# Hand-set waits and fixed buffers in place of a scheduler's pools, in a store-heavy batched product kernel

## Chip, cores, metric

The kernel runs on one core of one Trainium2 chip. The metric is the device time of one execution in microseconds (us), as the median of several. The engines are called TensorE (PE), VectorE (DVE), ScalarE (ACT), GpSimd (POOL) and SyncE (SP). SyncE only issues transfers. SBUF is the on-chip memory that transfers read and write, PSUM the memory that TensorE writes its products to.

## The reference

```python
def reference(x, y):            # both (8, 12, 512, 64), float32
    return np.einsum('bhtc,bhsc->bhts', x, y).astype(np.float32)   # (8, 12, 512, 512)
```

Two inputs of 12.6 MB each become 100.7 MB of output. Nothing can be stored in less than 125.83 MB of traffic in all.

## The kernel before

The inputs come in 12 loads of 2 MB (x and y of six groups of 16 heads), are cast to bf16 and rearranged by ScalarE, VectorE and GpSimd, and are transposed on VectorE. Then come 48 results of 2 MB each. A result is two groups of four products into one of two PSUM halves, two copies (evictions) by ScalarE into a slot in SBUF, and one store by SyncE. Five slots serve the loads and the stores in turn. A scheduler's pools hand out the buffers, and the scheduler sets the waits; the order is the program's. Cut to what matters:

```python
    slots = ctx.enter_context(tc.tile_pool(name="slots", bufs=SLOTS))   # SLOTS = 5
    tpool = ctx.enter_context(tc.tile_pool(name="tpool", bufs=2))
    pmpool = ctx.enter_context(tc.tile_pool(name="pmpsum", bufs=2, space=bass.MemoryType.PSUM))
    # ...
    def result(o, otf):                                   # otf: a slot
        i, h = divmod(o, V)
        xT, yT = made[i]
        ot = otf.rearrange("p (r s) -> p r s", s=S)
        for k in range(0, K, 4):
            pm = pmpool.tile([P, 4, S], fp32)
            for j in range(4):
                nc.tensor.matmul(pm[:, j, :], xT[:, k + j, h, :], yT[:, h * S:(h + 1) * S], start=True, stop=True)
            copy(nc.scalar, ot[:, k:k + 4, :], pm)
        nc.sync.dma_start(ov[i, h], otf)
    # ...
    with tc.manual_schedule():
        for g in range(SLOTS):
            load(g)
        for half, engine, part in ((0, nc.vector, 256), (1, nc.gpsimd, 128)):
            for k in range(0, K * E * D, part):
                engine.memset(zeroed[half][:, k:k + part], 0.0)
        # ... the front: 12 loads converted, results 0 to 3 among them
        for o in range(V, V * NH):                        # results 4 to 47
            result(o, slot())
            if o % V == V - 1:
                prepare(o // V + 2)                       # next transposes and rearrangements
```

## Time and profile before

| before | value |
|---|---|
| time, median of the 3 first runs | 301.13 us (301.11 to 301.54) |
| span of the profiled run | 299.4 us |
| TensorE / VectorE / ScalarE / GpSimd busy | 46 / 52 / 71 / 19 % |
| DMA engines busy by the kernel's queue | 98.8 % |
| read / written | 25.17 / 100.66 MB |

The table is read from the bottom: the busy share of every compute engine is far from 100, that of the DMA engines is not. The prediction shows the lines behind it. Here are only two more of the page before, of its third part (queue and kind: packets, MB, share of the 16 engines' span). They are the engines' own instructions, which are fetched by DMA too:

```profile
q8 instruction: 3, 0.05, 0.1%
q14 instruction: 3, 0.02, 0.0%
```

### The profile page before, as it was taken

The numbers are of one execution on the slowest core, as the hardware profiler recorded it, in microseconds if no ns is written. First come the engines' busy times: TensorE is split into PE (matmuls) and PEld (weight loads), VectorE is DVE, ScalarE is ACT, GpSimd is POOL, SyncE is SP. The second block draws the span as 40 slices with busy tenths as digits, with TensorE's granted clock in tenths as the row PEclk, the third lists the DMA queues.
The fourth block names the chain that finished last, engine by engine and source line by source line (L and its number), as shares of the span: only waits on it lengthen the run. The fifth ranks groups of instructions, "written<-read, shape, count | busy, mean of one in ns | idle before, by whom it ended". The sixth has DMA issues, their size and how long they took to land.

```text
span 299.4 us, 1218 instructions
## 1 busy us (share of the span) xinstructions
PE 136.7 (46%) x377; PEld 45.3 (15%) x384; DVE 154.5 (52%) x80; ACT 211.8 (71%) x109; POOL 56.6 (19%) x38
## 2 busy tenths in 40 slices
PE   0000130555665555746666466657465756465000
PEld 0000010111222221212112122212121212121000
DVE  2259996999749592916719359086192520000000
ACT  1756576999999978686867777777777686868100
POOL 3399989991000000000000000000000000000000
PEclk9999999978799997595677776677787577676555
DMA  7999999999999999999999999999999999999995
GB/s 282 431 433 429 429 427 431 429 425 436 431 427 433 431 425 430 440 424 427 440 425 427 442 422 429 437 425 431 427 431 429 425 429 425 429 422 427 429 431 219
DMA packets 8646, 125.91 MB, mean 421 GB/s; under 512 B 960, under 2 KB 960, under 8 KB 960
## 3 DMA queue, kind: packets, MB, share of 16 engines
q1 hardware_dynamic: 8640, 125.83, 98.8%
q8 instruction: 3, 0.05, 0.1%
q14 instruction: 3, 0.02, 0.0%
HBM read 25.17 MB, written 100.66 MB: 420 GB/s over the span
## 4 chain that ended last, share of the span: by engine, by line
DMA 55%; ACT 21%; DVE 7%; issue 5%; PE 2%; ACTq 1%; SPq 0%
DMA out_dram<-slot 48%; ACT slot L66 20%; DMA slot<-in_y_dram 7%; DVE yb L68 6%; PE pm L133 2%; DVE xT L115 1%; ACT yb L66 1%; ACTq L201 1%; DVE yT L120 1%; SPq L75 0%; ACTq L66 0%; ACT xk L83 0%
## 5 line engine op out<-in xcount | busy, mean ns | idle before, releaser
L66 ACT ACTIVATE slot<-pm 128x2048 f32<-128x2048 f32 x96 | 174.2, 1887 | 44.0 <-DMA out_dram<-slot 42.3
L133 PE MATMUL pm<-yT,xT 128*128 128x512 bf16 x377 | 136.7, 504 | 137.9 <-ACT slot L66 100.8
L115 DVE STREAM_TRANSPOSE xT<-xb 128x2048 uint32<-128x2048 uint32 x12 | 46.7, 3894 | 68.4 <-PE pm L133 68.3
L133 PEld LDWEIGHTS <-xT 128*128 128x128 bf16 x384 | 45.3, 118 | 228.5 <-issue 177.8
L68 DVE COPY xb<-xk 32x2048 bf16<-32x2048 bf16 x36 | 46.9, 1303 | 0.5
L68 DVE CAST yb<-slot 64x2048 bf16<-64x2048 f32 x12 | 38.5, 3204 | 16.8 <-DMA slot<-in_y_dram 16.6
L68 POOL COPY xb<-xk 32x2048 bf16<-32x2048 bf16 x12 | 37.3, 3107 | 9.6 <-ACT xk L83 8.9
L83 ACT ACTIVATE xk<-slot 128x4096 bf16<-128x4096 f32 x6 | 21.7, 3617 | 16.1 <-DMA slot<-in_x_dram 16.1
L120 DVE STREAM_TRANSPOSE yT<-yb 128x1024 uint32<-128x1024 uint32 x12 | 23.1, 1927 | 0.0
L66 ACT ACTIVATE yb<-slot 64x2048 bf16<-64x2048 f32 x6 | 14.8, 2462 | 5.1 <-DMA slot<-in_y_dram 5.1
L68 POOL CAST yb<-slot 64x2048 bf16<-64x2048 f32 x6 | 16.8, 2808 | 1.5 <-DMA slot<-in_y_dram 1.4
L152 DVE MEMSET xb<- 128x256 uint32 x8 | 2.2, 272 | 0.9 <-PEq L190 0.9
L152 POOL MEMSET xb<- 128x128 uint32 x16 | 2.3, 210 | 0.3 <-POOLq L190 0.3
L83 ACT ACT_TABLE_LOAD x1 | 1.3, 1283 | 0.7 <-PEq L190 0.7
L190 POOL MEMSET const-float32-0.0<- 128x1 f32 x1 | 0.1, 98 | 0.2 <-issue 0.2
L190 POOL MEMSET const-float32-1.0<- 128x1 f32 x1 | 0.1, 98 | 0.0
L190 POOL MEMSET const-bfloat16-1.0<- 128x1 bf16 x1 | 0.1, 98 | 0.0
L190 POOL MEMSET const-uint8-127<- 128x1 uint8 x1 | 0.1, 98 | 0.0
## 6 DMA issues: line engine op xcount, KB each, us to landing
out_dram<-slot SPq DMA_DIRECT2D x48, 2048.0 KB, 20.6
slot<-in_x_dram SPq DMA_DIRECT2D x6, 2048.0 KB, 16.4
slot<-in_y_dram SPq DMA_DIRECT2D x6, 2048.0 KB, 20.8
```

The lines of the kernel that those rows point to most:

```text
L66: nc.scalar.activation(dst, src, COPY)
L68: engine.tensor_copy(dst, src)
L83: nc.scalar.activation(xk.rearrange("p r c -> p (r c)"), src, COPY)
L115: nc.vector.transpose(xT.rearrange("p (k r e) -> p k e r", k=K, e=E), xb.rearrange("p (k e c) -> p k e c", k=K, e=E),)
L120: nc.vector.transpose(yT.rearrange("p (r j) -> p j r", r=D), yb.rearrange("p (j c) -> p j c", c=D))
L133: nc.tensor.matmul(pm[:, j, :], xT[:, k + j, h, :], yT[:, h * S:(h + 1) * S], start=True, stop=True)
L152: engine.memset(zeroed[half][:, k:k + part], 0.0)
L190: nc = _bacc.Bacc("TRN2", target_bir_lowering=False, num_devices=1)
L201: with _tile.TileContext(nc) as tc:
```

## The change

The intent is to wait for less. Each instruction says what it reads and writes; a small bookkeeping finds the points it depends on, drops those that its engine already knows to be past (also by way of another engine's knowledge), and sets the remaining waits by hand. The buffers are fixed and numbered. Each slot has its own DMA count. The two zeroings become one instruction each, results 43 and 47 are copied by VectorE, and everything stands in one section which the scheduler treats as a unit. All stores remain with SyncE. The core of the diff:

```diff
-    slots = ctx.enter_context(tc.tile_pool(name="slots", bufs=SLOTS))
-    pmpool = ctx.enter_context(tc.tile_pool(name="pmpsum", bufs=2, space=bass.MemoryType.PSUM))
+    slots = [sb.tile([P, K * S], fp32, name=f"slot{i}") for i in range(SLOTS)]
+    pms = [ps.tile([P, 4, S], fp32, name=f"pm{i}") for i in range(2)]
     # ... the same for all other buffers
+    def need(name, points):
+        best = {}
+        for p, v in points:
+            if known[name].get(p, 0) < v:
+                best[p] = max(best.get(p, 0), v)
+        for p, v in list(best.items()):
+            if any(snaps[q, w].get(p, 0) >= v for q, w in best.items() if q != p):
+                del best[p]
+        for p, v in best.items():
+            engines[name].wait_ge(sems[p], v)
+            known[name][p] = v
+            for q, w in snaps[p, v].items():
+                known[name][q] = max(known[name].get(q, 0), w)
     # ...
     def slot():
-        return slots.tile([P, K * S], fp32, name="slot")
+        made_slots.append(len(made_slots) % SLOTS)
+        return made_slots[-1]
     # ...
-            copy(nc.scalar, ot[:, k:k + 4, :], pm)
-        nc.sync.dma_start(ov[i, h], otf)
+            copy("dve" if o in late else "act", ot[:, k:k + 4, :], pms[pm], [("pm", pm)], [("slot", s, pm)])
+        store(o, s)                       # late = results 43 and 47
     # ...
-    with tc.manual_schedule():
+    with tc.tile_critical():
     # ...
+        for i, name in enumerate(("dve", "pool", "dve", "pe", "act")):
+            need(name, [(f"dma{i}", ticks[f"dma{i}"])])
```

## The prediction

> **What bounds the kernel now.** I began with the page's totals and its slices in time, because they say at once whether any engine can be the bound over the whole span. The slices' last two rows, and the DMA queue's row:
>
> ```profile
> DMA  7999999999999999999999999999999999999995
> GB/s 282 431 433 429 429 427 431 429 425 436 431 427 433 431 425 430 440 424 427 440 425 427 442 422 429 437 425 431 427 431 429 425 429 425 429 422 427 429 431 219
> ...
> q1 hardware_dynamic: 8640, 125.83, 98.8%
> ```
>
> The DMA engines are 90% busy or more in 38 of 40 slices; the first and the last slice alone are lower. No compute engine comes near: ScalarE, the busiest, has 211.8 us of 299.4 (71%). The one queue moves 125.83 MB. At the 430 GB/s of the long middle stretch (second listing, line 110 to 270) that is 125.83 / 0.430 = 292.6 us. So 292.6 of 299.4 us is bytes over a fixed rate, and 6.8 us is all that any change which keeps the bytes can touch.
>
> Where these 6.8 us lie I read from busy time by stretch, at the two ends (columns: stretch, its length, PE, PE load, VectorE, ScalarE, GpSimd busy with counts, granted clock, DMA share, GB/s):
>
> ```profile
> 0.00:1.00 1.00, 0.00 (x0) 0.00 (x0) 0.14 (x1) 0.27 (x1) 0.47 (x6) 1.00 0.00 0
> 1.00:2.00 1.00, 0.00 (x0) 0.00 (x0) 0.99 (x5) 1.00 (x1) 1.00 (x9) 1.00 0.95 180
> ...
> 50.00:70.00 20.00, 10.44 (x24) 3.24 (x24) 17.13 (x7) 19.68 (x11) 17.49 (x6) 0.83 1.01 428
> 70.00:90.00 20.00, 11.73 (x39) 4.18 (x40) 14.25 (x7) 19.77 (x12) 0.00 (x0) 0.91 1.00 429
> ...
> 110.00:270.00 160.00, 96.72 (x257) 31.45 (x260) 71.97 (x40) 118.45 (x66) 0.00 (x0) 0.71 1.01 430
> ...
> 290.00:295.00 5.00, 0.00 (x0) 0.00 (x0) 0.00 (x0) 0.00 (x0) 0.00 (x0) 0.50 0.99 419
> 295.00:298.00 3.00, 0.00 (x0) 0.00 (x0) 0.00 (x0) 0.00 (x0) 0.00 (x0) 0.50 0.26 109
> 298.00:299.40 1.40, 0.00 (x0) 0.00 (x0) 0.00 (x0) 0.00 (x0) 0.00 (x0) 0.50 0.00 0
> ```
>
> The start loses about 2.6 us: no byte in the first microsecond, then a ramp. The end loses about 3.8 us: from 295 to 298 only a quarter of the DMA engines still work, and from 298.3 the closing barrier runs. I also followed the landings of the last store over its 16 DMA engines as the trace records them: first at 295.82, last at 298.31 us. One engine lags by 2.5 us, and the kernel ends 1.08 us after it.
>
> Next the waits of the issuing queue, to see which waits the change could take away:
>
> ```profile
> SPq L137 <- ACT slot L66: 204.4, 48, 10.8
> SPq L75 <- DVE yb L68: 26.6, 3, 11.1
> SPq L201 <- DMA out_dram<-slot: 20.0, 1, 20.0
> ```
>
> SyncE waits 204.4 us for evictions, which looks like a bound and is not one. A store is issued while its predecessors are still in the DMA rings, and lands a median 20.6 us after issue, although 2 MB take only 2.097 / 0.430 = 4.88 us of the engines. So about four transfers are queued ahead of each store. The evictions wait for landings in turn:
>
> ```profile
> ACT slot L66 <- DMA out_dram<-slot: 42.3, 34, 1.7
> ```
>
> ScalarE is thus paced by the stores and not the stores by ScalarE. In the chain that ended last, stores carry 48% and evictions 20%: both halves of the ring of five slots, whose period in the second half is 20.8 us of landing plus 3.7 us of eviction, 24.5 us for five stores of 4.9 us each.
>
> **What the Trainium skill says.** "DMA: Bandwidth & Descriptors", section Specifications, gives a fabric ceiling of 435 GB/s for the 16 engines together. The trace agrees: 430 GB/s in the middle, 99% of it, for loads (4 to 50 us: 431) and stores alike. The same page, section Issuing engines are not separate DMA queues, says that transfers from all engines run on the same 16 DMA engines. So even the stores' place of issue would be no lever; here it stays SyncE anyway. "Runtime: NRT & Kernel Launch", section Instruction fetch mechanics, says that sequencers fetch instructions by DMA in 16 KiB blocks. The trace shows three packets of 16 KiB on one instruction queue, at 100, 174 and 253 us, and three of 8 KiB on another, smaller than the page's block. The packet at 100 us took 0.96 us, and the spread of landings went from 0.65 to 1.86 us there: these fetches make the lag at the end. For the late VectorE copies, "Perfetto Trace Analysis", section Optimizing Scalar/DVE Operations, gives some 125 ns of access overhead on PSUM for VectorE. No VectorE copy from PSUM is in this trace.
>
> **The change part by part.**
>
> 1. Waits by hand. In the built programs SyncE's instructions that only wait fall from 63 to 8, since each store after the third waited for an older transfer's count as well as for ScalarE. Such an instruction takes 17 ns by its record. Fifty-five of them are below 55 x 0.06 = 3.3 us of dispatch even at the 61 ns spacing the trace shows for back-to-back ones, and all lie inside the 204 us that SyncE idles. The older counts had been reached long before. ScalarE's go from 55 to 50, TensorE's rise from 3 to 13, VectorE's stay 17. On the path: 0.
>
> 2. Fixed buffers. Five slots, two products' halves in PSUM, two sets of transposed inputs, five or six kept ones: the same numbers in the same rotation, and the instruction order on all engines is the same but for the two points below. On the path: 0.
>
> 3. Zeroing in one instruction instead of 8 and 16. It ends by 3.1 us before; the first load lands at 8.3 us. On the path: 0.
>
> 4. The evictions of results 43 and 47 go to VectorE. VectorE's memset of 256 four-byte columns takes 272 ns in the trace; eight times that is 2.2 us, and with the page's overhead I estimate 2.3 us each against ScalarE's 1.88, so a store is issued about 0.8 us later. Ahead of it lie four transfers, 19.5 us. On the path: 0.
>
> 5. Entry to and exit from the hand-synchronized section. SyncE signals and branches once more before the first load: two sequencer instructions and a semaphore hop. The same kind of steps are about 60 ns apart in the trace, and SyncE needed 85 ns from barrier to first load; so +0.15 us, wholly on the path, as every byte moves with it. At the end five SyncE waits at 61 ns (0.31 us) go away. In their place come ScalarE's branch and drain, one hop, then two waits, a no-op and a branch on SyncE: six or seven steps, 0.4 us. So +0.1 us.
>
> 6. Instruction fetches. TensorE's listed instructions fall from 776 to 405, because a weight load is no longer a separate entry. I expect the machine program to have both as before, hence the same three 16 KiB fetches. SyncE's fall from 129 to 79, so one 8 KiB fetch may vanish or move: 8 KiB take 0.31 us of one engine, if it is the lagging one. -0.1 us on average.
>
> Sum: +0.15 + 0.1 - 0.1 = +0.15 us, so 301.13 + 0.15, rounded to 301.3 us.
>
> **The rivals.**
>
> First rival: the queue runs dry in the front. Between 54 and 90 us evictions and input conversions share ScalarE, which is busy 19.7 of 20 us in both stretches above. I took each store's issue against the first landing of its predecessor: at 68.0 us the cover is 3.5 us, at 78.0 us only 3.1 us, less the 1.0 us that lies between issue and first packet at the start. So 2 us of slack are left, where the steady state has 17. If a hand-set wait on GpSimd or VectorE delays the front by 3 us, the time rises by 1 us; a delay of 8 us, which would cost 2%, has no source in the diff. For it: GpSimd now waits for itself before each step. Against: ScalarE's order and durations there are unchanged, and the transposes on VectorE wait for TensorE or for casts there and not for GpSimd. It would make 302 to 303.
>
> Second rival: TensorE becomes the bound, if the weight loads can no longer run beside the products. 8 loads x 118 ns = 0.94 us per store, on top of 8 x 0.504 = 4.0 us at the average clock: 4.97 us against 4.88. That would add up to 0.1 us x 40 stores = 4 us in the worst case, but four queued transfers absorb it until late. Against it: ScalarE's wait for TensorE is 1.6 us in total now. It would make at most 303.
>
> Third rival: the waits removed were worth something, as the intent of the change suggests. Then the DMA engines would have to show gaps in the middle; they show 1.00 to 1.01 of share. Only the 6.8 us at the ends remain, and nothing in the diff shortens the ramp; an end with less lag could give 0.5 to 1 us. It would make 300.2.
>
> **Range and chances.** The three runs before lie within 0.43 us. With the lag at the end (up to 1 us either way) and the front rival upward, 300.4 to 302.3 should hold it 8 times in 10. Faster by over 2% means under 295.1, 5.9 of the 6.8 us that are not bytes: 1%. Slower by over 2% means over 307.2: 2%. Within 2%: 97%.
>
> **What would show it.** DMA share of 0.99 or more in all stretches from 4 to 290 us, and 430 GB/s; SyncE's wait for evictions again some 200 us although its wait instructions are gone; the first load issued at about 0.9 instead of 0.74 us; about 1.2 instead of 1.08 us from the last landing to the end; four VectorE copies of some 2.3 us near the end with nothing waiting for them. It is wrong if the DMA row shows a hole between 55 and 95 us (first rival), if ScalarE's wait for TensorE grows to tens of microseconds (second), or if the middle stretch moves more than 431 GB/s (then the rate, and not the waiting, had changed).

## The result, and the profile after

The changed kernel takes 300.99 us (median of 4 runs, 300.72 to 301.31); the kernel before, in the same rounds, 301.12 us (4 runs, 300.98 to 301.54). The ratio is 0.9994, 95% interval 0.9976 to 1.0011: the same. (A ratio here is the mean time of one kernel's fast runs over the mean of the other's of the same rounds, so not quite the ratio of the medians quoted.)

The slices' last two rows and the queues, from the page after:

```profile
DMA  7999999999999999999999999999999999999995
GB/s 270 430 430 438 425 425 427 434 427 430 427 438 427 430 432 432 429 427 432 434 427 435 430 430 430 430 430 427 434 430 423 430 434 419 432 423 425 430 434 248
...
q1 hardware_dynamic: 8640, 125.83, 98.9%
q8 instruction: 3, 0.05, 0.1%
q14 instruction: 2, 0.02, 0.0%
```

The row of the DMA engines is digit for digit that of before. One 8 KiB packet of instructions is gone from the second instruction queue. Busy time by stretch after, with the columns of the prediction's listing:

```profile
50.00:70.00 20.00, 9.99 (x24) 2.49 (x24) 17.28 (x7) 19.71 (x10) 18.10 (x6) 0.59 1.00 427
70.00:90.00 20.00, 11.69 (x41) 3.43 (x40) 13.97 (x7) 19.74 (x12) 0.00 (x0) 0.89 1.01 432
...
110.00:270.00 160.00, 98.69 (x260) 25.18 (x260) 76.88 (x42) 114.78 (x64) 0.00 (x0) 0.70 1.01 430
...
295.00:298.00 3.00, 0.00 (x0) 0.00 (x0) 0.00 (x0) 0.00 (x0) 0.00 (x0) 0.50 0.28 120
298.00:299.00 1.00, 0.00 (x0) 0.00 (x0) 0.00 (x0) 0.00 (x0) 0.00 (x0) 0.50 0.00 0
```

The middle stretch moves 430 GB/s again, and the front stretches have no hole. The waits of SyncE after (waited for: us in total, times, longest):

```profile
SPq L211 <- ACT slot L112: 189.4, 46, 6.6
...
SPq L211 <- DVE slot L114: 10.7, 2, 5.5
```

Together 200.1 us for 48 stores, against 204.4: SyncE has 55 fewer wait instructions and waits as long as before, since what it waits for comes no sooner. ScalarE still waits 45.2 us for stores to land (before 42.3).

What moved lies at the ends. First the issue of the first load, in the timeline of before and then of after (start, duration, engine, line, operation):

```profile
0.74 0.39 SPq L75 DMA_DIRECT2D slot<-in_x_dram  x1
```

```profile
0.95 0.39 SPq L130 DMA_DIRECT2D slot<-in_x_dram  x1
```

The landings of the last store over its 16 DMA engines complete the account (a landing is the moment at which one DMA engine reports its share of a transfer done); in the trace of before they come at 295.82 to 298.31 us, in that of after at 296.04 to 297.87 us:

| part of the span | before | after | change |
|---|---|---|---|
| first landing of the last store | 295.82 | 296.04 | +0.22 |
| from its first to its last landing (lag) | 2.49 | 1.83 | -0.66 |
| from the last landing to the end | 1.08 | 1.11 | +0.02 |
| span | 299.39 | 298.98 | -0.42 |

(Each entry is rounded by itself.) The later start of 0.22 us arrives unchanged at the first landing, 295 us later: everything between kept the rate. It is outweighed by a shorter lag of the last DMA engine. One profile of each is no proof of so small a difference; the timed runs say only that the sum is within 0.25%.

One thing I had not foreseen: the last two loads. Before, they were issued at 43.0 and 43.5 us, after at 41.7 and 51.5 us. The pool had given them the slots of loads 5 and 6, while the fixed rotation gives them those of loads 6 and 8, which come free later. It did no harm: at 51.5 us the load ahead of it had its first landing 5.5 us away (57.0 us), so the DMA rings did not run dry.

### The profile page after: what moved, and what is told of

Its sections match the earlier page's. It is cut to its first block, busy times and chain, and to the rows that moved or that the text cites. A ratio compares the mean times of both kernels' runs of the same rounds, so it can differ in the third digit from the quotient of the medians.

```text
span 299.0 us, 1170 instructions
## 1 busy us (share of the span) xinstructions
PE 138.6 (46%) x384; PEld 36.3 (12%) x384; DVE 160.8 (54%) x77; ACT 204.4 (68%) x105; POOL 56.1 (19%) x23
## 4 chain that ended last, share of the span: by engine, by line
DMA 62%; ACT 22%; issue 4%; DVE 3%; PE 1%; SPq 0%; ACTq 0%; DVEq 0%
DMA out_dram<-slot 48%; ACT slot L112 20%; DMA slot<-in_y_dram 7%; DMA slot<-in_x_dram 6%; DVE yb L114 2%; DVE slot L114 2%; PE pm L201 1%; ACT xk L112 1%; ACT yb L112 1%; SPq L130 0%; ACTq L80 0%; SPq L293 0%; DVEq L80 0%; SPq L234 0%
## 5 line engine op out<-in xcount | busy, mean ns | idle before, releaser
L201 PE MATMUL pm<-yT,xT 128*128 128x512 bf16 x384 | 138.6, 506 | 135.7 <-ACT slot L112 96.5
L112 ACT ACTIVATE slot<-pm 128x2048 f32<-128x2048 f32 x92 | 166.8, 1891 | 45.7 <-DMA out_dram<-slot 45.2
L201 PEld LDWEIGHTS pm<-yT,xT 128*128 128x128 bf16 x384 | 36.3, 115 | 237.1 <-ACT slot L112 136.8
L114 DVE CAST yb<-slot 64x2048 bf16<-64x2048 f32 x12 | 36.2, 3018 | 16.9 <-DMA slot<-in_y_dram 16.7
L114 POOL COPY xb<-xk 32x2048 bf16<-32x2048 bf16 x12 | 36.2, 3020 | 10.4 <-ACT xk L112 9.6
L114 DVE COPY slot<-pm 128x2048 f32<-128x2048 f32 x4 | 9.0, 2286 | 28.4 <-DMA out_dram<-slot 28.4
L114 POOL CAST yb<-slot 64x2048 bf16<-64x2048 f32 x6 | 17.8, 2972 | 1.4 <-DMA slot<-in_y_dram 0.8
L240 DVE MEMSET xb<- 128x2048 uint32 x1 | 1.8, 1765 | 1.4 <-SPq L234 1.4
L240 POOL MEMSET xb<- 128x2048 uint32 x1 | 1.8, 1804 | 0.5 <-SPq L234 0.5
```

The lines of the kernel that those rows point to most:

```text
L112: lambda: nc.scalar.activation(dst, src, COPY)
L114: else engines[name].tensor_copy(dst, src),
L201: last = nc.tensor.matmul(pms[k // 4][:, j, :], xT[:, k + j, h, :], yT[:, h * S:(h + 1) * S], start=True, stop=True,)
L240: lambda: engines[name].memset(xbs[half], 0.0),
```

## The experiments

Eleven more kernels ran. Theory A is the prediction's: the DMA engines' rate is the bound and the waits lie beside it. Each is given as its edit against the changed kernel or that of before.

### Every wait made anew

```diff
         best = {}
         for p, v in points:
-            if known[name].get(p, 0) < v:
-                best[p] = max(best.get(p, 0), v)
-        for p, v in list(best.items()):
-            ...                               # dropping what another point implies
+            best[p] = max(best.get(p, 0), v)
         for p, v in best.items():
             engines[name].wait_ge(sems[p], v)
-            known[name][p] = v
-            ...                               # taking over the other engine's knowledge
```

> The changed kernel with its knowledge of counts taken out: every instruction waits anew on everything it depends on, also where that is long known (instructions that only wait: 307 in place of 102 in the built program). Theory A (the DMA engines' rate is the bound, waits lie beside it): 301.0 +- 0.5 us, DMA share 1.00 or more in the middle, and the wait for evictions on SyncE still near 200 us. Rival B (unneeded waits cost time on the path, and the change gained by dropping them what it lost elsewhere): 205 more wait instructions at about 0.06 us are some 12 us if exposed; already a quarter of it would show as over 303 us.

Measured: 301.91 us (301.71 to 302.05), ratio to before 1.0022 (1.0007 to 1.0037), some 0.9 us over the changed kernel. Rival B's 3 us or more are not there, but theory A's 301.0 +- 0.5 is missed as well by 0.4 us. Its own waits do not explain this. SyncE's wait for ScalarE's evictions, and its queue of instructions fetched, in this run:

```profile
SPq L204 <- ACT slot L105: 190.3, 46, 6.6
```

```profile
q14 instruction: 4, 0.03, 0.0%
```

The wait is that of the changed kernel (189.4), and the first landing of the last store comes at 296.12 us against 296.04: until there nothing is lost. The rest is at the end: the last landing is 2.35 us after the first (1.83), and from there to the end it takes 1.59 us (1.11), of which 0.4 us is a pause of SyncE between two instructions of the closing section. So up to the first landing 205 wait instructions cost nothing measurable, and about 0.9 us arise at the end. That the longer program makes them is not shown by this run: of its four 8 KiB packets the last comes at 299.87 us, after the last landing, so only one more than in the changed kernel can have touched the lag. The runs on instruction fetches below follow up the lag; what makes SyncE's pause stays open. Only 7 of the 205 waits stand on SyncE (63 wait instructions before, 8 after, 15 here), so the 55 that the change took from SyncE are tested by before and after alone.

### Half the stores: what are the waits worth where the DMA rate is not the bound?

```diff
-        nc.sync.dma_start(ov[i, h], otf)
+        nc.sync.dma_start(ov[i, h, :, :, :K * S // 2], otf[:, :K * S // 2])
```

The same edit was made to the changed kernel and to that with every wait anew. The three results are wrong on purpose.

> The kernel before with each store cut to the first half of its columns (output wrong on purpose), so that 75.5 MB are moved and at 430 GB/s need 176 us: the DMA engines are no longer the bound. ScalarE should be: from the 78th us on, 3.54 us per result as in the stretch from 86 to 102 us of the full kernel, 43.5 results more, so 78 + 154 + about 6 us of last store and end = 238 us, DMA share near 0.7. It is there to be compared with the next two. If it stays near 300 us, the bound was not the DMA rate at all.

> The changed kernel with the same cut stores (output wrong on purpose). Theory A (the waits by hand are worth next to nothing even where ScalarE is the bound, since the waiting instructions stand beside a running copy): 3.51 us per result in place of 3.54, so 0.3 to 1 per cent faster than the half kernel of before, within 2 us of it. Rival B (they are worth something that the DMA rate hid): over 2 per cent faster than the half kernel of before, under 233 us if that one takes 238.

> The kernel of the first run (every wait made anew) with the cut stores (output wrong on purpose). Theory A: within 1 per cent of the changed kernel with cut stores, because the waits are already met and are dispatched beside a running copy. Rival B: 50 more waits on ScalarE at 0.06 us or more and 84 more on TensorE lie in the chain of copies and products: 3 to 8 us slower than it.

Measured: 236.08, 238.37 and 239.30 us. The first is near the 238 us expected, and it confirms the bound of the full kernel: with 40% of the bytes taken away, 65 us go (one wait went with them, as is shown below; it is worth 1.7 us). But the changed kernel is 2.3 us slower than that of before, where I expected it slightly faster. In the stretch from 110 to 200 us all three are alike (copies into the slots; columns: stretch, its length, VectorE, ScalarE, GpSimd busy, granted clock, DMA share, GB/s), in the order of the runs:

```profile
110.00:200.00 90.00, 0.00 (x0) 90.00 (x53) 0.00 (x0) 1.00 0.72 298
```

```profile
110.00:200.00 90.00, 0.00 (x0) 90.00 (x52) 0.00 (x0) 1.00 0.72 295
```

```profile
110.00:200.00 90.00, 0.00 (x0) 90.00 (x52) 0.00 (x0) 1.00 0.72 296
```

ScalarE is busy for 90.00 of 90 us in each, the DMA engines for 72%. A store is issued every 3.540 us in all three (before: from 90.65 us for result 8 to 211.01 us for result 42, 34 steps; the other two: the same 120.36 us). That is the clean reading of these runs: even with ScalarE as the bound, the hand-set waits gain nothing per store and 205 more waits cost nothing per store. In these runs the dispatch of the added waits lies beside a running copy. The 2.3 us arise elsewhere, and all before that stretch or after it. So does the 0.9 us by which the kernel with every wait anew is slower than the changed one: its last store is issued 0.43 us later, and the rest comes after that.

### Two guesses at the 2.3 us

Theory C held that the VectorE copies of results 43 and 47 cost them; rival D, that TensorE's weight loads do, since in the changed kernel they stand behind the wait of their product.

```diff
 # kernel of before, half stores
-            copy(nc.scalar, ot[:, k:k + 4, :], pm)
+            copy(nc.vector if o in (V * NH - V - 1, V * NH - 1) else nc.scalar, ot[:, k:k + 4, :], pm)
 # changed kernel, half stores
-    made_slots, loaded, late = [], {}, (V * NH - V - 1, V * NH - 1)
+    made_slots, loaded, late = [], {}, ()
```

> The half-store kernel of before (output wrong on purpose) with one part of the change alone: results 43 and 47 are copied by VectorE. In the half-store kernel of the change ScalarE idled 3.1 us at result 43, because VectorE held both halves of PSUM 2 x 2.24 us, and the last result took 4.49 us on VectorE. Theory C (the 2.3 us that the changed half kernel lost are these late copies, 1.9 to 2 us, and 0.2 to 0.3 us of a later start): 236.1 + 1.9 = 238.0 +- 0.4 us. Rival D (the loss comes from the weight loads, which now stand behind the wait of their product): 236.1 us, unchanged.

> The half-store kernel of the change (output wrong on purpose) with all evictions back on ScalarE. Theory C: 238.4 - 1.9 = 236.5 +- 0.4 us, that is the half kernel of before and the later start. Rival D: 238.4 us, unchanged.

Measured: 235.70 and 238.21 us, in other rounds and on another chip than the half runs; the kernel of before took 301.2 us in both. Theory C fell in both: the late copies cost nothing even here. I read this so that their 3.1 us of idle ScalarE at result 43 come back because ScalarE has two results fewer to copy.

Rival D met both numbers, but it does not fit the equal 3.540 us per store. So I looked for the place instead, and compared the issue times one by one. The gap of the two half kernels is 0.22 us at the first load, 0.36 us at the tenth, and 2.13 us from the first store on, where it stays. The first store in the two timelines, before and after:

```profile
52.85 0.65 SPq L137 DMA_DIRECT2D out_dram<-slot  x1
```

```profile
54.98 0.66 SPq L211 DMA_DIRECT2D out_dram<-slot  x1
```

My experiment had made this: the first half of a slot's columns is written by the first of its two evictions. The scheduler of before sees that and lets the half store go 1.8 us sooner; the bookkeeping of the change always waits for both. The next pair takes the middle half, which both evictions write:

```diff
-        nc.sync.dma_start(ov[i, h], otf)
+        nc.sync.dma_start(ov[i, h, :, :, K * S // 4:3 * K * S // 4], otf[:, K * S // 4:3 * K * S // 4])
```

> My half-store kernels were not alike. The first half of a slot's columns is written by the first of its two evictions, and the scheduler of before knows that: there the store waits for one eviction, while the changed kernel's bookkeeping waits for both (first store issued at 52.8 us against 55.0 in the half runs, after starts of 0.74 and 0.95). Here the store takes the middle half of the columns (output wrong on purpose), which both evictions write. Theory E (the 2.2 us between the half kernels are 1.8 us of this and 0.2 to 0.4 us of later start): 236.1 + 1.8 = 237.9 +- 0.4 us. Rival D (weight loads standing behind waits cost the changed kernel 2 us): still 236.1 us.

> The changed kernel with the same middle-half stores (output wrong on purpose). Its waits are those of the half run, so 238.4 +- 0.4 us by both theories; it is the partner of the run before, in the same rounds. Theory E: 0.1 to 0.3 per cent slower than that one. Rival D: 1 per cent slower.

Measured: 237.77 us (237.64 to 237.82) and 238.71 us (238.27 to 239.29). The kernel of before rose by 1.7 us as theory E said, and rival D fell. The first store is now issued at 54.86 and 55.07 us, 0.21 us apart, as are the first loads (0.74 and 0.96). The pair still differs by 0.9 us in the medians, more than the 0.1 to 0.3% expected (0.4%). The four runs of the changed kernel lie in two groups, at 238.3 to 238.4 and 239.0 to 239.3 us; the lower one fits the 0.2 us of later start plus 0.4, and the profiled run is of the upper one. In it, the gap to the kernel of before grows in steps of 0.3 us at single stores: one at the seventh (from 0.25 to 0.57 us), two more at the last two (0.35, 0.64, 0.94 us). What makes them is open; so in this pair the hand-set waits gain nothing, and some 0.7 us beyond the later start are unexplained.

### Instruction fetches and the lag at the end

The changed kernel, with drains (instructions that move no data) which GpSimd executes while it has nothing else to do:

```diff
         store(o, s)
+        if o >= V:
+            engines["pool"].wait_ge(sems["act"], ticks["act"])
+            for _ in range(32):
+                nc.gpsimd.drain()
```

> The changed kernel with 32 drains per result from the fifth on in GpSimd's program (1408 of them; GpSimd has nothing else to do by then), so that its instructions must be fetched: some 11 packets of 8 KiB more. Theory F (fetches delay the DMA engine that they run on, and this makes the lag of the last engine at the end): if they fall on one engine, 11 x 0.31 = 3.4 us more lag, first to last landing of the last store over 5 us, time 304; if they are spread over several, up to 1 us more lag and 301.3 to 302. Rival G (the lag has another cause): lag 1.8 us and time 301.0, as in the changed kernel.

Measured: 304.19 us (304.15 to 304.29), ratio 1.0098 (1.0084 to 1.0112). No engine that matters executes anything more, and no byte of data is added; the time rises by 3.2 us. The instruction queue, and the last stretches:

```profile
q14 instruction: 14, 0.11, 0.1%
```

```profile
295.00:296.00 1.00, 0.00 (x0) 0.00 (x0) 0.00 (x0) 0.00 (x0) 0.00 (x0) 0.50 0.81 344
...
298.00:299.00 1.00, 0.00 (x0) 0.00 (x0) 0.00 (x0) 0.00 (x0) 0.00 (x0) 0.50 0.11 49
299.00:300.00 1.00, 0.00 (x0) 0.00 (x0) 0.00 (x0) 0.00 (x0) 0.00 (x0) 0.50 0.11 49
300.00:301.00 1.00, 0.00 (x0) 0.00 (x0) 0.00 (x0) 0.00 (x0) 0.00 (x0) 0.50 0.04 16
```

One of the 14 packets has 32 bytes and comes at 0.1 us; the other 13 have 8 KiB, eleven more than in the changed kernel, as many as expected. At 296 us most DMA engines have finished as before, but from 298 to 300 us 0.11 of 16 engines, fewer than two, still work. The landings of the last store say the same: 14 of 16 by 297.81 us, the other two at 300.58 and 301.13. The lag grew from 1.83 to 4.98 us, 3.15 us for 11 packets, or 0.29 us each; each takes 0.31 us by its record. Rival G fell, and the number is that of theory F for one carrier.

But two engines are late by about 3 us each, while eleven packets of 0.31 us, shared between two engines, would make only 1.7 us on each. The landings of all stores show more. From 190 us on, the second-latest landing, counted from the store's first, jumps at each of the last five 8 KiB packets (at 191.7, 212.2, 232.1, 252.0 and 271.8 us) by 0.41 to 0.47 us, and falls a little between them. Read as one engine, this one is delayed by fetches, and it alone would have ended the last store at 300.58 us. The latest landing shows no such steps there; it creeps by some 0.1 us per store, from 3.3 us at the store of 174 us to 5.1 us at that of 272 us. So theory F is shown for one of the two engines; what slows the other, which ends the kernel 0.55 us later still, is open.

### Which engines lag?

The kernel with the added drains, and after its last store:

```diff
+        for j, r in enumerate((1, 2, 4, 8, 12, 14, 15, 16)):     # after the last store, same queue
+            ... nc.sync.dma_start(mark[0:r, j * 128:(j + 1) * 128], xv[0, 0:r, 0:128]) ...
```

> Which DMA engine lags? The kernel with GpSimd's added drains (14 fetches of 8 KiB, 5.0 us of lag) with eight small loads after the last store on the same queue, of 1, 2, 4, 8, 12, 14, 15 and 16 rows into a tile nobody uses any more. The Trainium skill says that a transfer over k engines takes the k lowest-numbered ones; if so, each lands when the slowest of its engines has worked off the last store: about 296.5 us without the lagging engine, about 301.3 us with it. All theories hold that the lag is one engine's; I expect it among the engines 8 to 15 (so that the loads of 2, 4 and 8 rows land near 296.5 us), without a reason that any run shows. The result tells whether a last store that leaves this engine out can end the kernel sooner.

Measured (one look, 305.9 us): the landings that the trace records agree with k engines for k rows, as "DMA: Bandwidth & Descriptors" has it in its section Why a DMA increments its semaphore by 16 and not by 1: one landing for one row, two for two rows, four for four, besides one that is recorded at the issue of each load of fewer than 16 rows. The load of 2 rows has both at 296.6 and 296.8 us. The load of 4 rows has three by 296.96 and one at 300.56. The load of 8 rows has that one and a second late one, at 301.47; those of 12 to 16 rows have the same two and no third. So if the numbering holds, one lagging engine is among numbers 2 and 3 and the other among 4 to 7. My expectation (8 to 15) was wrong. It also closes the way I had in mind to a faster kernel: a last store that leaves the lagging engines out can't be had from SyncE, if fewer engines means the low ones, as that section says.

### The ramp at the start

The zeroings of the changed kernel were made to wait for the first load:

```diff
         for half, name in enumerate(("dve", "pool")):
+            need(name, [("dma0", 16)])
             emit(
```

> The changed kernel with the two zeroings held back until the first load has landed (they are needed at 12 us and take 1.8 us). Of the 2 MB of that load the first landing comes at 8.06 and the last at 8.69 us, while bytes alone from the first packet at 1.97 us would need 4.88 us: 1.2 to 1.8 us are lost in the ramp. Theory M (the zeroing on VectorE and GpSimd slows the first packets): the first conversion on ScalarE starts at 7.6 us or earlier in place of 8.71, and the time falls by 0.5 to 1 us. Rival N (the ramp belongs to the transfers themselves): it starts at 8.7 +- 0.1 us and the time stays 301.0 +- 0.4 us. I hold N for likelier, 3 to 1.

Measured: 301.01 us (300.94 to 301.24), ratio to before 0.9994 (0.9980 to 1.0008). The first conversion on ScalarE in this run, and in the changed kernel, from their timelines:

```profile
8.67 3.62 ACT L112 ACTIVATE xk<-slot 128x4096 bf16<-128x4096 f32 x1 [6.49 <-DMA slot<-in_x_dram]
```

```profile
8.71 3.62 ACT L112 ACTIVATE xk<-slot 128x4096 bf16<-128x4096 f32 x1 [6.52 <-DMA slot<-in_x_dram]
```

Equal within 0.04 us: rival N holds. The zeroing is not what slows the first load.

## Why the prediction was right

**The bound.** It said that 292.6 us are bytes over a fixed rate, and that nothing in the change alters either. The rate stayed 430 GB/s, and the half-store runs showed that it is the bytes that set the time. This is why a change that rewrites all synchronization moved the time by less than the noise.

**Step 1, the waits (0).** Right. 205 more waits left the first landing of the last store where it was (296.12 against 296.04 us), and with ScalarE as the bound all variants issued a store every 3.540 us. The expected gain did not go into a new wait: SyncE's waits that were taken away had been met before they were asked, for each of the 48 stores of before was released by ScalarE, as the line of 204.4 us shows, and none by an older transfer.

**Step 2, the buffers (0).** Right in time, wrong in its reason. It claimed the same rotation; the last two loads sit in other slots, and one was issued 8 us later. A cover of 5.5 us hid it, which the prediction had not worked out: here the zero was luck. In another kernel such a shift could have been the result.

**Step 3, the zeroing (0).** Right, also when it was moved behind the first load.

**Step 4, the late copies (0).** Right: nothing on the path. They took 2.29 us each (estimate 2.3), in this group of the profile after:

```profile
L114 DVE COPY slot<-pm 128x2048 f32<-128x2048 f32 x4 | 9.0, 2286 | 28.4 <-DMA out_dram<-slot 28.4
```

That the size fits is partly luck. The estimate counted eight memsets of 272 ns, 2.2 us; the one memset over the same 2048 columns in the profile after took 1.77 us. So a copy from PSUM cost 0.5 us more than a memset of its width, and not the 0.1 us that the estimate added.

**Step 5, entry and exit (+0.25).** The sum came out: +0.22 us at the entry where it said +0.15, +0.02 at the exit where it said +0.1. Each term was off by 0.07 or 0.08 us, and the two misses cancel, which is luck.

**Step 6, the fetches (-0.1).** The direction was right and the size too small: the lag was 0.66 us shorter in the one trace. Four traces bear on it. With three 8 KiB packets before the last landing the lag was 2.49 us (before) and 2.35 us (every wait anew); with two it was 1.83 us (after) and 1.86 us (zeroing held back). In the trace of before, the packet at 188.7 us moved the latest landing of a store from 1.89 to 2.38 us behind its first, more than the 0.31 us that it takes by its record. The rest of a lag is not steps: in the same trace the second-latest landing crept from 0.73 to 1.59 us between the stores of 101 and 169 us. So the prediction's "these fetches make the lag" holds in part, and its "one engine lags" too, for another landed late as well, at 297.61 us. The change of the lag was the largest term of all, which I had not expected. So the sum was -0.13 us by the medians (-0.42 us by the two spans) in place of +0.15, all inside the range; four runs of each kernel can't tell so small a sum from zero, so its sign is neither a hit nor a miss.

**The rivals.** The front did not run dry: the cover was 3.3 us at 68.3 us and 2.9 us at 78.4 us, as tight as before. One transpose on VectorE did wait 2.4 us for GpSimd in the profile after, which the prediction had ruled out; it started at 31.2 us in place of 30.9, 0.2 us of which is the later start, and no hole followed. TensorE did not become the bound: ScalarE waited 0.4 us for it in all. The third rival's mechanism, waits worth something, was refuted by the runs; but its figure of an end with less lag is what happened in small.

## What to carry to other kernels

Before removing waits, ask what the waiting engine would do next if it did not wait: here it would join a queue that was already four transfers deep, and 204 us of waiting on SyncE were worth nothing. When DMA engines are full from end to end, only the first and the last microseconds can be moved. In this kernel even instructions of an engine with nothing else to do, 1408 drains, counted there, with 3.2 us. And an experiment that shrinks a transfer must keep its dependencies: my half stores lacked one wait in one of the two kernels, which looked like a 1% difference between them.

## What the Trainium skill lacked or had wrong

- "Runtime: NRT & Kernel Launch", section Instruction fetch mechanics, calls the cost of crossing a block mostly hidden; it speaks of the sequencer that fetches, and leaves out what the fetch takes from the DMA engines. In this DMA-bound kernel 1408 drains on an idle engine, with 11 more fetches of 8 KiB, cost 3.2 us (304.19 against 300.99 us), 0.29 us for each fetch. The page also has blocks of 16 KiB alone; three of 16 KiB and two or three of 8 KiB were fetched here.
- No page has which DMA engines carry the fetches. In the kernel with the drains two of 16 ended late, at 300.6 and 301.1 us against 297.8 us or earlier for the other 14; one is among numbers 2 and 3 and one among 4 to 7, if small transfers take the lowest-numbered engines. Steps of 0.41 to 0.47 us at five fetches show up in the landings of one of them alone.
- No page has how far the DMA engines stay below their rate in the first microseconds. In the trace of before they moved 180, 164 and 262 GB/s in the second, third and fourth microsecond, against 430 later. In the changed kernel the first load of 2.097 MB landed between 8.06 and 8.69 us after a first packet at 1.97 us, 1.2 to 1.8 us later than at 430 GB/s (4.88 us), and holding back the zeroing on VectorE and GpSimd did not change it.
